# Paddings, earlier fetches, an unprioritised attention and a sum on GpSimd in a two-layer decoder step

## The chip, the cores and the metric

The kernel runs on one NeuronCore of a Trainium2 chip. The metric is the device time of one execution in microseconds; a kernel's number is the median of its runs. A core has five engines with their own instruction queues: TensorE (PE) for matrix products, with weight loads shown apart as PEld; VectorE (DVE); ScalarE (ACT); GpSimd (POOL); and SyncE (SP), which here issues nearly all DMA transfers.

## The reference

One inference step of a trunk with two layers, in fp32, for a prompt of 16 meta tokens and 256 tokens and for a sample group of 8 sequences with one new token each: 280 tokens in all. D is 2048, the branch width 4096, heads have 64 values. Cut to what matters:

```python
# layer A (RWKV-7), xm = token-shifted mixes of rmsnorm(h)
r, k, v, z = rkvz products of 2048 x 4096 each
kk = k * k_k;  kk = kk / max(sqrt(sum(kk * kk, over each head)), 1e-12)
S = S * d - (S kk) b^T + v k^T;  y = S r            # per token and head
y = groupnorm(y) * gn_g + gn_b + sum(r * k * r_k) * v
h = h + (y * silu(z)) @ w_out
# shared K/V, then layer B: window of 128, 64 query heads on 8 K/V heads, one sink per head
k, v = split(rmsnorm(h, kv_norm) @ w_kv);  k = rotary(k)
q, z = split(rmsnorm(h, b_norm) @ b_w_qz);  q = rotary(q)
m = max(max(s), sink);  p = exp(s - m) / (sum(exp(s - m)) + exp(sink - m))
h = h + ((p @ v) * silu(z)) @ b_w_o
y = rmsnorm(h, final_norm)
```

The sample group attends to a cache of 128 keys and values per sequence and K/V head and returns the cache moved on by one.

## The kernel before

**Products.** Every large product is computed to near fp32 from operands split in two: `hi` is the value rounded to the fast format (fp32r), `lo` the rest. `mm3` (lines 199 to 201) issues three TensorE products per block: weight-hi by input-hi, weight-hi by input-lo, weight-lo by input-hi. Tokens are the moving side (280 columns, 264 in layer B, where the meta tokens are dropped), the weights the stationary 128x128 side. `wunits` brings the weights in units of 256 KB: a DMA on SP into a `raw` tile (line 192), a cast on ACT to `whi` (line 177), a subtraction on DVE to `wlo` (line 178). There are 4 `raw` buffers, 4 more (`rawx`) once a wider pool is open, and 5 of `whi` and `wlo`. `gate_tiles` splits the gated branch in the same way, eight tiles `at[g]` of 128x1056 into `ghi` and `glo`, as the input of an output product.

**Order of the work.** TensorE's order is written by hand. `drive` runs a generator of products, six TensorE products to each `yield` (a *position*), and between positions it advances *streams* that emit other work: a stream's `yield n, condition` says how many positions to wait and for what. What a stream emits on TensorE stands in TensorE's queue exactly there. The instructions of the other engines and the DMA issues are put into their queues by a scheduler that simulates the program and has a priority per instruction; `drive` emits the second stream under a priority raised by 2000, the others at the normal one. Once made, each queue runs in order.

**Stages.** In the trace: layer A's products with the chunked recurrence (64 tokens a chunk) in the streams, to about 1345 us; the rest of layer A's output product, to 1460; the shared K/V (`phase_b`), to 1518; layer B's q and z products with the attention of 8 groups in the stream `heads` (`phase_b2`, `products_b`), then z products alone, to 2015; the output product `out_b`, to 2211; final norm and output.

**Names that the change touches.** `ps_kk` (lines 484 and 777): sums of squares of k per head, as two accumulating fp32 products whose stationary side `sel` has 4 columns of a selection matrix; the result stands in 4 rows. An fp32 product shows as two records of the trace. `ps_yt` (line 1210): transpositions of the recurrence's result Y, three blocks of tokens per head pair, 128, 128 and 16 rows. `ps_vt` (lines 488 and 794) transposes v in the other direction, with 128, 128 and 16 columns. `km` (line 843): a factor of k, on ACT. `snk`, `snd` (lines 1490 and 1495): the sinks, spread over partitions, one load and eight small ones. `kc`, `vc` (lines 1706 and 1707): the cached keys and values of one K/V head, and with them the copies that move the output cache on (line 1711), four issues per group, emitted by `attend_cache` at the start of each group. `scores_b`, `softmax` (DVE and ACT, ending in the scaling `P<-P,sm`, line 1667), `turned` (transpositions of P, `ps_pt`, line 1676) and `values` are a half group's attention; `heads` runs 16 of these pairs. `end_z` (line 1545 on) makes the gated branch of one 128-column plane out of a z product. In `out_b`, h is the sum of product and residual (line 1784), `ps_h` its transposition (line 1787), `ht` the scaled result, `junk` and `ss` its squares summed along a row by ACT (line 1792), `rsf` the row's sum and then its root's inverse.

Of the kernel before, what the change touches and what calls it, by code (L numbers as in the profile page):

```python
# [103 lines left out]
class Kernel:  # L104
# [9 lines left out]
    def run(self):  # L114
        nc, tc = self.nc, self.tc
        with contextlib.ExitStack() as st:
# [32 lines left out]
            self.close("gB", "st1", "wx1", "g0", "at", "res")  # L149
# [92 lines left out]
    def params(self):  # L242
# [27 lines left out]
        for off, n in ((C_SEL, 8), (C_BO, 128)):  # L270
            self.cr[off] = self.cp.tile([128, n], F32, name=f"cr{off}")
            dma(self.cr[off], I['consts'][:, off:off + n])
        self.sel = self.cr[C_SEL]
# [194 lines left out]
    def proj(self, m, x, pairs, dst, gemm=None):  # L468

        nc = self.nc  # L470
        for p0 in pairs:
# [5 lines left out]
            for j, ps in enumerate(pss):  # L477
                nc.scalar.copy(t[:, j], ps)
                if m == 1:
                    sq = self.sp.tile([128, N], F32, tag="sqp", bufs=1, name=f"sqp{p0}_{j}")  # L480
                    nc.scalar.activation(sq, ps, AF.Square, scale=self.pcol(P_KK, p0 + j))
                    if j == 0:
                        pk = self.bank(self.py, f"ps_kk{p0}")
                    nc.tensor.matmul(pk[:4, :N], self.sel[:, 4 * j:4 * j + 4], sq, start=j == 0, stop=j == 1)
# [79 lines left out]
    def drive(self, products, streams, begun):  # L564
# [5 lines left out]
        with self.pe_order():  # L570
            while more or self.later or len(live) > 1:
                for s in list(live):
                    if s[1] <= self.pos and (s[2] is None or s[2]()):
# [3 lines left out]
                        try:  # L577
                            with self.tc.high_priority(offset=2000 if s[0] is now[1] else 0), turn:
# [190 lines left out]
    def end_k(self, p0, t):  # L769
# [6 lines left out]
        for j in range(2):  # L776
            nc.tensor.matmul(pk[:4, :N], self.sel[:, 4 * j:4 * j + 4], sq[:, j], start=j == 0, stop=j == 1)
# [22 lines left out]
    def prep(self, u):  # L800
# [41 lines left out]
        for j in range(2):  # L842
            km = rp.tile([128, N], F32, tag="km", name=f"km{j}_{u}")
# [348 lines left out]
    def group_norm(self, o):  # L1192
# [10 lines left out]
        for j in range(4):  # L1203
# [4 lines left out]
            for c in range(3):  # L1208
                r = 128 if c < 2 else 16
                nc.tensor.transpose(ps[:, 128 * c:128 * c + r], Y[:r, c, j].rearrange("p q i -> p (q i)"),  # L1210
                                    self.ident[:r, :r])
# [193 lines left out]
    def phase_b(self):  # L1405
# [11 lines left out]
        self.Vn = t([128, NKV, 2, 64], "Vn")  # L1417
        G.memset(self.Vm, 0.0)
# [60 lines left out]
    def phase_b2(self):  # L1479
# [9 lines left out]
        snk = t([128, 64], "snk")  # L1489
        dma(snk, I['b_sinks'].to_broadcast((128, 64)))  # L1490
        snd = t([128, NKV], "snd")
        G.memset(snd, 0.0)
        with nc.allow_non_contiguous_dma(reason="64 values"):
            for s in range(NS):
                dma(snd[8 * s:8 * s + 8], I['b_sinks'][0].rearrange("(g h) -> h g", h=8))
        self.snk, self.snd = snk, snd
# [8 lines left out]
        self.drive(self.products_b(), [idle(), self.heads()], {})  # L1505
# [42 lines left out]
    def end_z(self, g, pl, ps):  # L1548
# [10 lines left out]
        V.scalar_tensor_tensor(at, zr, 0.5, at, op0=MU, op1=MU)  # L1559

    def heads(self):

        last = None
        for n in range(16):
            g, i = divmod(n, 2)
            if i == 0:
                cache = self.attend_cache(g)
                next(cache)
# [4 lines left out]
            P = [self.softmax(g, 2 * i + a, ps) for a, ps in enumerate(cur)]  # L1573
            yield 4, self.after(3, ('q', g, 3))
            next(cache)
# [3 lines left out]
            next(cache, None)  # L1579
            yield 3  # L1580
# [8 lines left out]
        self.st1 = self.open("st1", side="right", reuse_waits="tile")  # L1589
        self.plan_states(self.st1, 12, [*range(10, 42, 8), *range(64, 176, 7)], 5)  # L1590

# [175 lines left out]
    def out_b(self):  # L1767
        nc, pool, I, O = self.nc, self.gp, self.I, self.O
        V, A = nc.vector, nc.scalar
        gates = [self.gate_tiles(pool if g else self.gp0, NB, g, self.at[g]) for g in range(8)]  # L1770
# [5 lines left out]
        ss = pool.tile([128, 3, KT], F32, name="ss")  # L1776
        V.memset(ss, 0.0)
        for k in range(KT):
# [5 lines left out]
            V.tensor_tensor(h, ps, self.hT[:, k, NM:], op=ALU.add)  # L1784
            pt = self.bank(self.pe, f"ps_h2_{k}")
            for i, r in enumerate(rows):
                nc.tensor.transpose(pt[:r, 128 * i:128 * i + 128], h[:, 128 * i:128 * i + r], self.ident)  # L1787
            for i, r in enumerate(rows):
                s = slice(128 * k, 128 * k + 128)
                V.tensor_tensor(ht[i][:r, s], pt[:r, 128 * i:128 * i + 128], fn[:r, s], op=ALU.mult)  # L1790
                j = pool.tile([128, 128], F32, tag="junk", bufs=2, name=f"junk{k}_{i}")
                A.activation(j[:r], pt[:r, 128 * i:128 * i + 128], AF.Square, accum_out=ss[:r, i, k:k + 1])
        rs = pool.tile([128, 3], F32, name="rsf")
        V.reduce_sum(rs, ss, axis=AX.X)
# [34 lines left out]
```

## Time and profile before

| | |
|---|---|
| median of 3 runs | 2229.13 us (2228.17 to 2234.97) |
| profiled execution, its own time | 2228.68 us |
| its span, first to last instruction | 2226.9 us |
| mean granted TensorE clock | 0.989 |
| busy: PE, PEld, DVE, ACT, POOL | 96%, 90%, 77%, 58%, 3% |
| moved by DMA | 455.40 MB, 205 GB/s mean |

How to read the rows: a timeline row has its start and length in us, the engine, the line of the kernel, the operation, the tile written and the tiles read, the tile's shape (for PE and PEld first rows*columns of the stationary side) and how many such instructions stand in a row; in brackets stands how long the engine was idle before and what ended that. `SPq` is the queue of SP: the length of its rows is the time until the next instruction could be issued. A group's row has its count, busy time and mean in ns, then the idle time before. The granted clock is the share of TensorE's full speed.

### The profile page before, as it was taken

To read this page: it belongs to the slowest core of one execution; us is meant where nothing else is said; L and a number is where in the kernel's file an instruction comes from. 1 tells how busy PE (TensorE), PEld (TensorE's weight loads), DVE (VectorE), ACT (ScalarE), POOL (GpSimd) and SP (SyncE) were. 2 spreads that over 40 slices of the span, in tenths; PEclk is the share of its full clock that TensorE was granted. 3 is DMA by queue.
4 is the path that set the end of the run, shared out by engine and by line. 5 is a ranking of instruction groups with operands and counts; after the bars stand their busy time and mean duration, and the time that the engine had idled before them with its cause. 6 is when DMAs were issued, how large, how long until landed. Compare 5 with 4: busy or idle time off the path is not lost. (4 is left out here: it accounts for less than half of the span.)

```text
span 2226.9 us, 56386 instructions
## 1 busy us (share of the span) xinstructions
PE 2129.4 (96%) x21584; PEld 2000.4 (90%) x21584; DVE 1715.0 (77%) x4136; ACT 1295.2 (58%) x3041; POOL 63.4 (3%) x86
## 2 busy tenths in 40 slices
PE   6999999999999999999999999998999999999997
PEld 4898888899899898989989999998989999999997
DVE  5875757787777777788887787996878888778785
ACT  3546766677666666667666454564556555545443
POOL 0010000000000000000100000100000000000000
PEclk9999999999999999999999999998999999999998
DMA  7978577668666766866656768766544544576773
GB/s 240 339 257 251 179 225 217 201 177 263 211 199 189 225 210 198 262 210 183 194 164 199 242 203 263 242 189 195 153 141 138 169 126 143 165 218 218 229 226 129
DMA packets 424887, 455.40 MB, mean 205 GB/s; under 512 B 64281, under 2 KB 383321, under 8 KB 424225
## 3 DMA queue, kind: packets, MB, share of 16 engines
q1 hardware_dynamic: 423800, 449.51, 65.1%
q8 instruction: 169, 2.77, 0.5%
q10 hardware_dynamic: 816, 2.29, 0.3%
q14 instruction: 102, 0.83, 0.1%
HBM read 385.09 MB, written 70.73 MB: 205 GB/s over the span
## 5 line engine op out<-in xcount | busy, mean ns | idle before, releaser
L199 PE MATMUL ps_q<-bmh,whi_qb 128*128 128x264 f32 x512 | 151.9, 297 | 8.0 <-ACT whi_qb L177 7.9
L199 PE MATMUL ps_z<-mhlm,whi_z 128*128 128x280 f32 x512 | 159.2, 311 | 0.0
L201 PE MATMUL ps_z<-mhlm,wlo_z 128*128 128x280 f32 x512 | 150.2, 293 | 0.5 <-DVE wlo_z L178 0.4
L201 PE MATMUL ps_q<-bmh,wlo_qb 128*128 128x264 f32 x512 | 147.6, 288 | 3.0 <-DVE wlo_qb L178 3.0
L200 PE MATMUL ps_z<-mhlm,whi_z 128*128 128x280 f32 x512 | 150.0, 293 | 0.0
L201 PE MATMUL ps_z<-bmh,wlo_zb 128*128 128x264 f32 x512 | 146.4, 286 | 2.7 <-DVE wlo_zb L178 2.7
L199 PE MATMUL ps_z<-bmh,whi_zb 128*128 128x264 f32 x512 | 148.2, 289 | 0.8 <-ACT whi_zb L177 0.8
L201 PE MATMUL ps_ob<-ghi,wlo_ob 128*128 128x264 f32 x512 | 145.5, 285 | 3.1 <-DVE wlo_ob L178 3.1
L200 PE MATMUL ps_q<-bml,whi_qb 128*128 128x264 f32 x512 | 146.8, 287 | 0.0
L200 PE MATMUL ps_ob<-glo,whi_ob 128*128 128x264 f32 x512 | 144.6, 283 | 1.3 <-DVE glo L178 1.3
L200 PE MATMUL ps_z<-bml,whi_zb 128*128 128x264 f32 x512 | 145.6, 284 | 0.0
L199 PE MATMUL ps_ob<-ghi,whi_ob 128*128 128x264 f32 x512 | 144.9, 284 | 0.0
L178 DVE TENSOR_TENSOR wlo_r<-raw_r,whi_r 128x512 fp32r<-128x512 f32 x128 | 86.9, 686 | 58.3 <-ACT whi_r L177 56.1
L177 ACT CAST whi_oa<-raw_oa 128x512 fp32r<-128x512 f32 x128 | 78.6, 622 | 88.7 <-DMA raw_oa<-a_w_out 29.9
L178 DVE TENSOR_TENSOR wlo_v<-raw_v,whi_v 128x512 fp32r<-128x512 f32 x128 | 87.4, 689 | 51.4 <-ACT whi_v L177 45.6
L177 ACT CAST whi_ob<-raw_ob 128x512 fp32r<-128x512 f32 x128 | 79.1, 621 | 78.1 <-PE ps_ob L200 59.3
L199 PE MATMUL ps_v<-mhlm,whi_v 128*128 128x280 f32 x384 | 121.7, 317 | 0.2 <-ACT st L734 0.2
L199 PE MATMUL ps_k<-mhlm,whi_k 128*128 128x280 f32 x384 | 118.8, 309 | 0.0
L178 DVE TENSOR_TENSOR wlo_k<-raw_k,whi_k 128x512 fp32r<-128x512 f32 x112 | 76.6, 690 | 53.8 <-ACT whi_k L177 49.7
L177 ACT CAST whi_zb<-raw_zb 128x512 fp32r<-128x512 f32 x128 | 78.4, 622 | 65.0 <-PE ps_z L200 45.3
L178 DVE TENSOR_TENSOR wlo_z<-raw_z,whi_z 128x512 fp32r<-128x512 f32 x128 | 87.8, 690 | 36.7 <-ACT whi_z L177 36.3
L200 PE MATMUL ps_v<-mhlm,whi_v 128*128 128x280 f32 x384 | 112.2, 292 | 0.0
(473 smaller groups left out, 7707.1 us busy)
## 6 DMA issues: line engine op xcount, KB each, us to landing
raw_k<-a_w_rkvz SPq DMA_DIRECT2D x128, 256.0 KB
raw_v<-a_w_rkvz SPq DMA_DIRECT2D x128, 256.0 KB
raw_r<-a_w_rkvz SPq DMA_DIRECT2D x128, 256.0 KB
raw_z<-a_w_rkvz SPq DMA_DIRECT2D x128, 256.0 KB
raw_oa<-a_w_out SPq DMA_DIRECT2D x128, 256.0 KB
raw_qb<-b_w_qz SPq DMA_DIRECT2D x128, 256.0 KB
raw_zb<-b_w_qz SPq DMA_DIRECT2D x128, 256.0 KB
raw_ob<-b_w_o SPq DMA_DIRECT2D x128, 256.0 KB
```

The source lines that it names most:

```text
L177: self.nc.scalar.copy(hi, src)
L178: return self.nc.vector.tensor_tensor(lo, src, hi.bitcast(F32), op=ALU.subtract)
L199: mm(ps, wh, xh, start=start, stop=False)
L200: mm(ps, wh, xl, start=False, stop=False)
L201: return mm(ps, wl, xh, start=False, stop=stop)
```

## The change

It has five parts.

1. **Layer A.** `sel` becomes two windows, 128 columns wide, on a 130-column tile that is zero (memset on GpSimd) but for two columns; the `ps_kk` products now write 128 rows, of which 4 are read as before. The third transposition of `ps_yt` takes all 128 rows of Y and writes 128 columns, of which 16 are read. `km` uses the buffers of tag `sq`.
2. **Sinks and caches.** The nine loads of the sinks and a memset move from `phase_b2` to the start of `phase_b`. The first cache set is requested 12 positions into layer B's products; each later one at the end of the group before.
3. **Attention.** `drive` has a parameter `ahead`, 0 for layer B, so that `heads` has no priority. The second softmax of a pair is emitted four positions later, behind the `yield 4`.
4. **Gates.** A third stream, `gates_b`, splits the tiles `at[0]` to `at[4]` while the last z products run, each four positions behind its z planes; 5 to 7 stay in `out_b`.
5. **Final squares.** In `out_b` one Square of h on ACT per 128 columns of D replaces three reads of `ps_h` with a sum each; GpSimd adds the squares up in `sqacc`, and six small products with a column of ones (`ps_stb`) sum over the partitions at the end. Three instructions on DVE take the place of a reduction and one instruction.

```diff
+        selt = self.cp.tile([128, 130], F32, name="selt")
+        nc.gpsimd.memset(selt, 0.0)
+        dma(selt[:, 2:4], I['consts'][:, C_SEL:C_SEL + 2])
+        self.sel = [selt[:, 2:130], selt[:, 0:128]]
...
-            nc.tensor.matmul(pk[:4, :N], self.sel[:, 4 * j:4 * j + 4], sq[:, j], start=j == 0, stop=j == 1)
+            nc.tensor.matmul(pk[:, :N], self.sel[j], sq[:, j], start=j == 0, stop=j == 1)
...
-            km = rp.tile([128, N], F32, tag="km", name=f"km{j}_{u}")
+            km = rp.tile([128, N], F32, tag="sq", bufs=2, name=f"km{j}_{u}")
...
-                r = 128 if c < 2 else 16
-                nc.tensor.transpose(ps[:, 128 * c:128 * c + r], Y[:r, c, j].rearrange("p q i -> p (q i)"),
-                                    self.ident[:r, :r])
+                nc.tensor.transpose(ps[:, 128 * c:128 * c + 128], Y[:, c, j].rearrange("p q i -> p (q i)"), self.ident)
...
+        self.snk, self.snd = t([128, 64], "snk"), t([128, NKV], "snd")
+        dma(self.snk, I['b_sinks'].to_broadcast((128, 64)))
+        G.memset(self.snd, 0.0)
+        with nc.allow_non_contiguous_dma(reason="64 values"):
+            for s in range(NS):
+                dma(self.snd[8 * s:8 * s + 8], I['b_sinks'][0].rearrange("(g h) -> h g", h=8))
...
-        self.drive(self.products_b(), [idle(), self.heads()], {})
+        self.drive(self.products_b(), [idle(), self.heads(), self.gates_b()], {}, 0)
...
     def heads(self):
-        last = None
+        last, cache = None, self.attend_cache(0)
+        yield 12
+        next(cache)
         for n in range(16):
             g, i = divmod(n, 2)
-            if i == 0:
-                cache = self.attend_cache(g)
-                next(cache)
             yield (5 if n else 0), self.after(3, ('q', g, 2 * i + 1))
             cur = [self.scores_b(g, 2 * i + a) for a in range(2)]
             if last:
                 self.values(*last)
-            P = [self.softmax(g, 2 * i + a, ps) for a, ps in enumerate(cur)]
+            P = [self.softmax(g, 2 * i, cur[0])]
             yield 4, self.after(3, ('q', g, 3))
+            P.append(self.softmax(g, 2 * i + 1, cur[1]))
             next(cache)
             yield 8
             T = [self.turned(g, 2 * i, P[0])]
             yield 2
             next(cache, None)
+            if i and g < 7:
+                cache = self.attend_cache(g + 1)
+                next(cache)
...
+    def gates_b(self):
+        self.gates = []
+        for g in range(5):
+            yield 3, self.after(4, ('h', 7), ('z', g))
+            self.gates.append(self.gate_tiles(self.g1 if g else self.gp0, NB, g, self.at[g]))
...
-        gates = [self.gate_tiles(pool if g else self.gp0, NB, g, self.at[g]) for g in range(8)]
+        gates = self.gates + [self.gate_tiles(pool, NB, g, self.at[g]) for g in range(5, 8)]
...
+            sq = pool.tile([128, NB], F32, tag="sqb", bufs=2, name=f"sqb{k}")
+            A.activation(sq, h, AF.Square)
+            if k == 0:
+                acc = pool.tile([128, NB], F32, name="sqacc")
+                nc.gpsimd.tensor_copy(acc, sq)
+            elif k < KT - 1:
+                nc.gpsimd.tensor_tensor(acc, acc, sq, op=ALU.add)
...
-                A.activation(j[:r], pt[:r, 128 * i:128 * i + 128], AF.Square, accum_out=ss[:r, i, k:k + 1])
+            if k >= KT - 2:
+                for i, r in enumerate(rows):
+                    nc.tensor.matmul(pst[i][:r, 0:2], (acc if k == KT - 2 else sq)[:, 128 * i:128 * i + r], one,
+                                     start=k == KT - 2, stop=k == KT - 1)
...
-        V.reduce_sum(rs, ss, axis=AX.X)
-        V.tensor_scalar(rs, rs, 1.0 / D, EPS, op0=ALU.mult, op1=ALU.add)
+        for i, r in enumerate(rows):
+            V.tensor_scalar(rs[:r, i:i + 1], pst[i][:r, 0:1], 1.0 / D, EPS, op0=ALU.mult, op1=ALU.add)
```

How the queues change is seen in three places. The first is SP's queue at the start of layer B's products, between two loads of q weights (`raw_qb`). Before:

```order
L192 DMA raw_qb_2_23367<-b_w_qz 128x2x256
L1706 DMA kc_23233<-cache_k 128x8x64
L1707 DMA vc_23234<-cache_v 128x8x64
L1711 DMA s_cache_k<-cache_k 16x4064
L1711 DMA s_cache_v<-cache_v 16x4064
...
L1468 DMA s_cache_v<-Vn 8x8x64
L1490 DMA snk<-b_sinks 128x64
L1495 DMA snd<-b_sinks 8x8x1 x8
L192 DMA raw_qb_4_23379<-b_w_qz 128x2x256
```

Left out are the second cache set, four issues as in the first, and two of three transfers of K/V results: 20 issues in all stand between the two weights. After the change:

```order
L192 DMA raw_qb_2_23368<-b_w_qz 128x2x256
L1470 DMA Vm<-Vm 16x8x64
L1473 DMA p_cache_v<-Vd 128x512
L1475 DMA s_cache_v<-Vn 8x8x64
L1719 DMA kc_23362<-cache_k 128x8x64
L1720 DMA vc_23363<-cache_v 128x8x64
L1724 DMA s_cache_k<-cache_k 16x4064
L1724 DMA s_cache_v<-cache_v 16x4064
L192 DMA raw_qb_4_23380<-b_w_qz 128x2x256
```

Seven issues are left there; three more weights (`raw_qb_6`, `raw_qb_8`, `raw_qb_10`) follow, and only then the second cache set. The sinks' nine issues now stand in the K/V stage, behind `constb` and ahead of the next loads of K/V weights.

The second is ACT's queue at the turn from the z products (`thb` is `end_z`'s Tanh) to the output product (`whi_ob`). Before:

```order
L1556 ACTIVATE thb_2_30294<-zr_2_30292 128x264
L177 CAST whi_ob_6_30411<-raw_ob_6_30409 128x512
L177 CAST whi_ob_8_30441<-raw_ob_8_30439 128x512
L177 CAST ghi_30330<-at_23195 128x1056
L177 CAST ghi_30334<-at_23196 128x1056
L177 CAST ghi_30338<-at_23197 128x1056
L177 CAST ghi_30342<-at_23198 128x1056
L177 CAST ghi_30346<-at_23199 128x1056
L177 CAST ghi_30350<-at_23200 128x1056
L1556 ACTIVATE thb_3_30312<-zr_3_30310 128x264
```

After:

```order
L1555 ACTIVATE thb_2_30318<-zr_2_30316 128x264
L177 CAST whi_ob_6_30418<-raw_ob_6_30416 128x512
L177 CAST whi_ob_8_30448<-raw_ob_8_30446 128x512
L177 CAST ghi_30350<-at_23212 128x1056
L177 CAST ghi_30354<-at_23213 128x1056
L1555 ACTIVATE thb_3_30336<-zr_3_30334 128x264
```

Six gate casts in a row have become two; gates 1 to 4 stand earlier, among the casts of the z weights, and the last comes eight casts later.

The third is TensorE's queue at the end, after the change (`h_14` and `h_15` are the last two blocks of h):

```order
L1808 MATMUL ps_h_14_33011<-consts,h_14_33006 128x128 x2
L1808 MATMUL ps_h_14_33011<-consts,h_14_33006 8x128
L1814 MATMUL ps_stb_30367<-one,sqacc 128x2
L1814 MATMUL ps_stb_30368<-one,sqacc 128x2
L1814 MATMUL ps_stb_30369<-one,sqacc 8x2
L1808 MATMUL ps_h_15_33025<-consts,h_15_33021 128x128 x2
```

The small products that read GpSimd's sum stand between the two groups of transpositions; three that read the last square follow behind them. In layer B's q and z products TensorE's order is the same before and after; on DVE and ACT one to three casts of weights now stand ahead of a softmax's last scalings and exponentials.

More of the change, by code (lines that the diff above doesn't have):

```diff
@@ L148, in run @@
             self.wx = None
-            self.close("gB", "st1", "wx1", "g0", "at", "res")
+            self.close("gB", "g1", "st1", "wx1", "g0", "at", "res")
     def open(self, name, bufs=1, **k):
@@ L269, in params @@
         self.cr = {}
[L270 to L273, printed above, removed]
+        self.cr[C_BO] = self.cp.tile([128, 128], F32, name="crbo")
+        dma(self.cr[C_BO], I['consts'][:, C_BO:C_BO + 128])
+        selt = self.cp.tile([128, 130], F32, name="selt")
+        nc.gpsimd.memset(selt, 0.0)
+        dma(selt[:, 2:4], I['consts'][:, C_SEL:C_SEL + 2])
+        self.sel = [selt[:, 2:130], selt[:, 0:128]]
         self.half = self.cp.tile([128, 2], F32, name="half")
@@ L483, in proj @@
                         pk = self.bank(self.py, f"ps_kk{p0}")
-                    nc.tensor.matmul(pk[:4, :N], self.sel[:, 4 * j:4 * j + 4], sq, start=j == 0, stop=j == 1)
+                    nc.tensor.matmul(pk[:, :N], self.sel[j], sq, start=j == 0, stop=j == 1)
                 if m == 2:
@@ L559, in phase_a, with drive @@
                    {preps: [wait, need]})
-    def drive(self, products, streams, begun):
+    def drive(self, products, streams, begun, ahead=2000):
         self.samples = False
@@ L577, in drive @@
                         try:
-                            with self.tc.high_priority(offset=2000 if s[0] is now[1] else 0), turn:
+                            with self.tc.high_priority(offset=ahead if s[0] is now[1] else 0), turn:
                                 w = next(s[0])
@@ L1488, in phase_b2 @@
         V.tensor_scalar(self.sinr, self.sinr, HD ** -0.5, None, op0=MU)
[L1489 to L1496, printed above, removed]
         self.Pm, self.qz = t([128, 4, 128], "Pm"), [t([128, 576], f"qz{i}") for i in range(2)]
@@ L1588, in heads @@
         self.close("B2")
-        self.st1 = self.open("st1", side="right", reuse_waits="tile")
+        right = dict(side="right", reuse_waits="tile")
+        self.st1 = self.open("st1", **right)
         self.plan_states(self.st1, 12, [*range(10, 42, 8), *range(64, 176, 7)], 5)
+        self.g1 = self.open("g1", **right)
+    def gates_b(self):
[3 more added lines that the diff above has]
+            self.gates.append(self.gate_tiles(self.g1 if g else self.gp0, NB, g, self.at[g]))
     def bx(self, k):
@@ L1775, in out_b @@
         ht = [pool.tile([128, D], F32, name=f"ht{i}") for i in range(3)]
-        ss = pool.tile([128, 3, KT], F32, name="ss")
-        V.memset(ss, 0.0)
+        pst = [self.bank(p, f"ps_stb{i}") for i, p in enumerate((self.pc, self.pp, self.py))]
+        one = pool.tile([128, 2], F32, name="one")
+        V.memset(one, 1.0)
         for k in range(KT):
```

4 lines of the change are left out of this document (3 added, 1 removed).

## The prediction

> **What bounds the kernel now.** I read the page's busy shares first, then a table by stage, then what TensorE (PE) waits for, then the places themselves.
>
> ```profile
> PE 2129.4 (96%) x21584; PEld 2000.4 (90%) x21584; DVE 1715.0 (77%) x4136; ACT 1295.2 (58%) x3041; POOL 63.4 (3%) x86
> 1600.00:1700.00 100.00, 97.30 (x813) 92.94 (x811) 81.31 (x303) 57.09 (x154) 0.00 (x0) 0.98 0.47 143
> 1900.00:2000.00 100.00, 100.00 (x832) 99.40 (x831) 77.89 (x157) 50.92 (x102) 0.00 (x0) 1.00 0.64 191
> ```
>
> In the table a row has the stretch, its length, then busy time of PE, weight loads (PEld), DVE, ACT and GpSimd (POOL), the granted clock, the DMA share and GB/s. TensorE bounds the whole: 96% of the span, 97% in a stretch of the attention, 100% in the gate products. Two things alone can shorten it: less time per PE instruction, or fewer of the short stretches in which PE waits. The change goes after both. Where PE waits, in layer B:
>
> ```profile
> PE ps_z L201 <- DVE wlo_zb L178: 2.7, 4, 1.3
> PE ps_q L201 <- DVE wlo_qb L178: 3.0, 4, 1.3
> PE ps_q L199 <- ACT whi_qb L177: 7.9, 2, 7.5
> PE ps_ob L201 <- DVE wlo_ob L178: 3.1, 1, 3.1
> PE ps_ob L200 <- DVE glo L178: 1.3, 1, 1.3
> ```
>
> (microseconds in all, times, longest). Each names the split of a weight or a gate: ACT rounds it (whi, ghi), DVE subtracts (wlo, glo), and what PE multiplies next is not ready.
>
> **Layer A paddings.** What these cost is read from how long a foreign instruction interrupts the regular products, 0.12 to 0.13 us apart.
>
> ```profile
> 403.91 0.29 PE L201 MATMUL ps_v<-mhlm,wlo_v 128*128 128x280 f32 x1
> 404.50 0.29 PE L200 MATMUL ps_v<-mhlm,whi_v 128*128 128x280 f32 x1
> 408.42 0.29 PE L201 MATMUL ps_v<-mhlm,wlo_v 128*128 128x280 f32 x1
> 408.86 0.13 PEld L1210 LDWEIGHTS ps_yt<-consts,Y 16*128 16x128 f32 x1 [0.17 <-issue]
> 409.26 0.29 PE L200 MATMUL ps_v<-mhlm,whi_v 128*128 128x280 f32 x1
> 329.96 0.29 PE L201 MATMUL ps_k<-mhlm,wlo_k 128*128 128x280 f32 x1
> 331.22 0.19 PEld L199 LDWEIGHTS ps_k<-mhlm,whi_k 128*128 128x128 f32 x1 [0.47 <-issue]
> 331.45 0.29 PE L200 MATMUL ps_k<-mhlm,whi_k 128*128 128x280 f32 x1
> 99.40 0.29 PE L201 MATMUL ps_v<-mv,wlo_v 128*128 128x280 f32 x1
> 99.53 1.10 PE L402 MATMUL ps_a_w<-mst,lw 128*96 128x280 f32 x4
> 100.60 0.29 PE L200 MATMUL ps_v<-mv,whi_v 128*128 128x280 f32 x1
> L794 PEld LDWEIGHTS ps_vt<-consts,st x72: 88/138/143, 403.9 to 928.4; 128*128 128x128 f32 x48, 128*16 128x16 f32 x24
> L1210 PEld LDWEIGHTS ps_yt<-consts,Y x96: 132/138/143, 408.4 to 1350.2; 128*128 128x128 f32 x64, 16*128 16x128 f32 x32
> L777 PEld LDWEIGHTS ps_kk<-sqk,cr x48: 82/86/87, 330.2 to 843.8; 128*4 128x4 f32 x48
> L484 PEld LDWEIGHTS ps_kk<-sqp,cr x16: 82/84/86, 55.3 to 105.7; 128*4 128x4 f32 x16
> ```
>
> The last four rows count loads by shape, rows * columns (nanoseconds least/median/most). From the product before to the second product behind, the three transpositions of a vt group, 128 rows in each load, take 404.50 - 403.91 = 0.59 us; those of a yt group, 16 rows in the third, 409.26 - 408.42 = 0.84 us, and its load stands 0.17 us waiting for nothing shown. I put the 0.25 us on the 16 rows: 32 groups, 8.0 us. The pair of fp32 products with 4 columns takes 331.45 - 329.96 = 1.49 us, the pair with 96 columns 100.60 - 99.40 = 1.20; the load behind the first waits 0.47 us. So 0.29 a pair: 48 loads are 12 pairs (four a pair, as fp32 shows two records each), 3.5 us, and the 16 of phase 0 are 8 single products at, say, the same (each is followed by its own change back), 2.3 us. In all 13.8 us. I take 80%, **-11**: some of these breaks lie shortly ahead of a chain for which PE then waits, and the saving ends there. Against it: the vt group's own third load has only 16 columns and shows no pause, so narrow columns might not be what the pair pays for; that leaves the yt part alone, and two thirds of it are 5. Ends: -14 and -5.
>
> [...]
>
> [...] The memset of the wider matrix (GpSimd, ahead of all) and `km` taking the place of `sq` cost nothing: POOL is 3% busy, and ACT, which does both, 58%.
>
> **Sinks moved into the K/V stage.**
>
> ```profile
> 1463.05 8.43 SPq L192 DMA_DIRECT2D raw_kv<-w_kv  x2
> 1528.95 3.18 SPq L1495 DMA_DIRECT2D snd<-b_sinks  x8
> ```
>
> Nine issues at 3.18 / 8 = 0.40 us are 3.6 us on SP, put in ahead of 1463.05. There two weight loads take 8.43 us to issue, where eight issues took 3.18: they wait for a buffer that an earlier product must free, and that wait covers the nine. **+0.5** for loads a little late; all 3.6 if that cover is gone.
>
> **Start of layer B's products.**
>
> ```profile
> 1518.47 1.73 SPq L1706 DMA_DIRECT2D kc<-cache_k  x1
> 1530.77 0.28 PE L201 MATMUL ps_q<-bmh,wlo_qb 128*128 128x264 f32 x1
> 1532.23 16.04 SPq L192 DMA_DIRECT2D raw_qb<-b_w_qz  x11
> 1537.85 0.62 ACT L177 CAST whi_qb<-raw_qb 128x512 fp32r<-128x512 f32 x1 [4.63 <-DMA raw_qb<-b_w_qz]
> 1538.52 0.59 PE L199 MATMUL ps_q<-bmh,whi_qb 128*128 128x264 f32 x1 [7.48 <-ACT whi_qb L177]
> 1538.00:1548.00 10.00, 8.06 (x32) 7.22 (x33) 7.76 (x24) 7.46 (x24) 0.00 (x0) 0.50 0.43 133
> 1548.00:1558.00 10.00, 10.00 (x84) 10.00 (x84) 7.21 (x20) 4.33 (x7) 0.00 (x0) 1.00 0.65 197
> ```
>
> Twenty issues stand in SP's queue from 1518.47 to 1532.23, 13.76 us or 0.69 each, between two weight loads. The next weight is issued at 1532.23 and lands at 1537.85, 5.6 us later; PE has run dry at 1531.05 and stands 7.48 us, and once more 0.4 (7.9 in two waits, above). Then the clock: 0.50 from 1538 to 1548, 32 products instead of 84. Beside idle time it costs (84 x 0.806 - 32) x 0.12 = 4.3 us, 0.806 being the busy share of that stretch; I take 3.4, as part of that stretch has no product ready anyway. Together 7.9 + 3.4 = 11.3 us. After the change 7 issues stand there, by 0.69 each 4.8 us: the weight is issued at 1523.3 and lands at 1528.9, ahead of 1531.05, so neither the wait nor the lower clock should come. I leave 1.5 us, since the second cache set (4 issues, 2.8 us by 0.69) follows four weights later: **-9.8**, ends -11.3 (all gone) and -4 (the wait cut to half, but the clock still falls).
>
> **The rest of the attention.** The second softmax goes behind four positions, and no instruction is lifted ahead of the casts.
>
> ```profile
> 1863.11 0.55 DVE L1667 TENSOR_SCALAR P<-P,sm 128x128 f32<-128x128 f32 x2
> 1867.60 0.60 PE L1676 MATMUL ps_pt<-consts,P 128*128 128x128 f32 x4
> ```
>
> Beside the start PE waits for DVE's splits 2.7 + 3.0 = 5.7 us in eight places, one of them right behind the start. I read them so: a softmax's instructions, lifted by the priority, overtake the split that PE wants next, and DVE, 81% busy from 1600 to 1700, doesn't catch up in time. Of the 5.7 us I take **-4.5**, ends -6 (a little of the clock with it) and 0: without the lift a burst on DVE remains. What hides the later softmax is its slack: P is ready at 1863.66 and its transposition starts at 1867.60, 3.9 us later, the tightest of those I read. On DVE one to three splits go ahead of it, 0.7 us each, so 2 us of that is used.
>
> **Gates split early.**
>
> ```profile
> 2015.42 5.95 ACT L177 CAST ghi<-at 128x1056 fp32r<-128x1056 f32 x6
> 2021.01 3.59 DVE L178 TENSOR_TENSOR glo<-at,ghi 128x1056 fp32r<-128x1056 f32 x3
> ```
>
> Six casts stand in a row on ACT for 5.95 us, and the weights' splits behind them: PE waits 1.3 + 3.1 = 4.4 us. Four of these move into the gate products, where each is 0.99 us on ACT (50.92 of 100 busy) and 1.2 us on DVE (77.89): the idle 22% covers 4.8 us spread over some 100. Two casts are left at the turn. **-3.5**, ends -4.4 and -1.
>
> **Squares summed on GpSimd.**
>
> ```profile
> 2210.85 0.43 DVE L1784 TENSOR_TENSOR h<-ps_ob,hT 128x264 f32<-128x264 f32 x1 [1.01 <-PE ps_ob L201]
> 2215.04 0.20 DVE L1794 TENSOR_REDUCE rsf<-ss 128x3 f32<-128x48 f32 x1 [0.43 <-ACT junk L1792]
> L1388 POOL TENSOR_TENSOR sqacc<-sqacc,sqa 128x280 f32<-128x280 f32 x14 | 14.4, 1032 | 73.6 <-ACT sqa L1383 73.4
> ```
>
> Only the end counts: in the output products PE waits nowhere but in the two places at the turn, so the work that changes there runs beside PE. If DVE stood through all 14 sums on POOL, some 14.4 us, it would still have time: the idle 22% of the gate products' row, over 196 us, is 43. Before, ACT and DVE take turns on the same banks, the last wait of 0.43 us among them, and the reduction starts 2215.04 - 2211.28 = 3.8 us behind the last h. After, the path is a square (of the size of h, 0.43), three transpositions (as in layer A, 0.59 less the 0.12 of a product), three scalings of half that size, at most 0.3, and three short instructions of 0.2: 2.4 us if none overlaps. The new matmuls for the sum wait for GpSimd's last addition, about 1.03 us, in front of the last transpositions, which gives some back. 3.8 - 2.4 = 1.4, one short instruction less, and a little given back: **-1.5**, ends -2.2 and 0 (an addition of 1.7 us or more).
>
> **Sum.** -11 + 0.5 - 9.8 - 4.5 - 3.5 - 1.5 = -29.8 on the profiled execution's 2228.68: 2198.9, so **2199 us**; the three timed runs have their median 0.45 us higher, which is nothing here.
>
> **Rivals.** (1) The paddings bring nothing:
>
> ```profile
> L893 PEld LDWEIGHTS ps_bo<-rk,cr 128*128 128x128 f32 x64 | 10.0, 188 | 3.6 <-DVE vT L894 1.9 <-DVE ks L779 1.3
> ```
>
> A wide fp32 load in 128 columns is 188 ns in this group, a narrow one 85; if loads stood bare, 64 x 0.10 = +6.6 us, and with the pause kept the paddings end between 0 and +6.6 instead of -11: 2210 to 2217. For it: the 16-column load without a pause; against: the two breaks. (2) The start of B only shifts its stall to the second cache set, or the clock still falls: 4 to 8 us of the 9.8 stay, 2203 to 2207. For it: SP still has 11 issues there that are no weights; against it: four weights now go between them. (3) Both: 2214 to 2225. (4) Slower: without priority the softmax falls behind the splits; PE, in order, stands at `turned`. It decides from a slip over 3.9 us on; with ten splits of 0.69 ahead it is 6.9, a wait of 3 us on each of 15 pairs, +45 against the other terms' -29.8 + 4.5: 2248. Against it stand the one to three splits that moved. (5) The priority was not what made the waits, and gates and tail bring half: 2228.68 - 29.8 + 4.5 + 2.5 = 2206.
>
> **Chances.** The forecast 0.60, (1) 0.11, (2) 0.14, (3) 0.05, (4) 0.04, (5) 0.06. All lower ends together are -37.9, 2191; of the upper ones I let the two largest fall together, -5 and -4 in place of -11 and -9.8, 2211: its own range. Rivals 2 and 5 lie in it and 1 just above, so 2188 to 2216 holds 8 in 10, with the misses of my sizes. A measurement here tells no change apart to about 0.3%, 6.7 us: faster means under 2222.4. All but (4) and about half of (3) fall there: faster 0.92, same 0.04, slower 0.04.
>
> **What would show it.** Paddings: breaks of the yt group near 0.59 us, of the kk pair near 1.2, layer A's end some 11 us earlier. Start: no PE wait over 2 us from 1500 to 1560 (less the shift), granted clock 1.0 there. Attention: PE's waits on `wlo_qb` and `wlo_zb` under 2 us together, none of a transposition of P on DVE. Gates: no wait on `wlo_ob` at the turn. End: the first rsf step at most 2.5 us behind the last h. It would be wrong if breaks stay as they are, or if a softmax row appears as PE's releaser.

## The result, and the profile after

The changed kernel takes 2209.15 us (median of 4 runs, 2203.19 to 2211.88), the kernel before 2232.05 us beside it (4 runs, 2228.17 to 2240.49): the ratio is 0.9885, with a 95% interval of 0.9864 to 0.9907, about 26 us less. Later comparisons, with more runs of the kernel before, put that one at 2234 to 2235 us. The profiled execution of the changed kernel took 2211.88 us, the one of before 2228.68.

The first products of the shared K/V, of q and of the output product mark the stages. In both traces (a tile's instructions: count, least/median/most ns, first and last start), before:

```profile
L199 PE MATMUL ps_kv<-kvh,whi_kv x128: 287/292/399, 1456.8 to 1513.3; 128*128 128x280 f32 x128
L199 PE MATMUL ps_q<-bmh,whi_qb x512: 279/285/586, 1513.7 to 1855.7; 128*128 128x264 f32 x171
L199 PE MATMUL ps_ob<-ghi,whi_ob x512: 278/283/373, 2014.8 to 2210.3; 128*128 128x264 f32 x171
```

and after:

```profile
span 2209.9 us, 56367 instructions
PE 2122.6 (96%) x21596; PEld 2013.0 (91%) x21596; DVE 1711.5 (77%) x4138; ACT 1283.1 (58%) x2961; POOL 76.1 (3%) x102
L199 PE MATMUL ps_kv<-kvh,whi_kv x128: 287/291/399, 1462.6 to 1520.5; 128*128 128x280 f32 x128
L199 PE MATMUL ps_q<-bmh,whi_qb x512: 279/284/422, 1520.9 to 1846.5; 128*128 128x264 f32 x171
L199 PE MATMUL ps_ob<-ghi,whi_ob x512: 278/283/378, 2004.8 to 2195.3; 128*128 128x264 f32 x171
```

From the first K/V product to the end it is 2226.9 - 1456.8 = 770.1 us before and 2209.9 - 1462.6 = 747.3 after: 22.8 us less behind layer A. Layer A itself ended 5.8 us *later* in this execution, though it was to end 11 us earlier. Both halves need an answer. Matching every product of one trace with the same product of the other gives the shift along the way:

```
at (trace of before)     shift of the same product in the changed kernel
 393 us  layer A          +0.8
 444     layer A          +5.6
1457     shared K/V       +5.8
1519     first q products +7.2     K/V stage  +1.4
1596     q, attention     -1.2     start      -8.4
1920     z alone          -10.0    attention  -8.9
2044     output product   -14.9    gates      -4.9
2227     end              -17.0    tail       -2.1
```

**Layer A's breaks** are as short as forecast (timeline; a product, the foreign instruction, the second product behind):

```profile
409.23 0.29 PE L201 MATMUL ps_v<-mhlm,wlo_v 128*128 128x280 f32 x1
409.36 0.49 PE L1212 MATMUL ps_yt<-consts,Y 128*128 128x128 f32 x3
409.82 0.29 PE L200 MATMUL ps_v<-mhlm,whi_v 128*128 128x280 f32 x1
330.79 0.29 PE L201 MATMUL ps_k<-mhlm,wlo_k 128*128 128x280 f32 x1
330.92 1.11 PE L780 MATMUL ps_kk<-sqk,selt 128*128 128x280 f32 x4
332.00 0.29 PE L200 MATMUL ps_k<-mhlm,whi_k 128*128 128x280 f32 x1
L780 PEld LDWEIGHTS ps_kk<-sqk,selt x48: 188/189/190, 330.8 to 849.3; 128*128 128x128 f32 x48
```

A yt group takes 0.59 us (0.84 before), a kk pair 1.21 (1.49), and over all such breaks the median is 0.59, 1.20 and, for the single kk products of phase 0, 0.73 (1.02). The kk loads did become longer, 189 ns for 86, and the break shorter all the same.

**Layer B's waits** are nearly gone. PE's list of waits between 1500 us and the end of the z products, after, and the granted clock in the stretches that answer to those before:

```profile
PE ps_q L199 <- ACT whi_qb L177: 1.8, 1, 1.8
PE ps_q L201 <- DVE wlo_qb L178: 1.1, 3, 0.5
...
1540.00:1560.00 20.00, 17.30 (x127) 16.66 (x126) 15.35 (x52) 10.90 (x31) 0.00 (x0) 0.91 0.62 187
1600.00:1700.00 100.00, 99.77 (x853) 96.04 (x852) 84.40 (x311) 58.84 (x155) 0.00 (x0) 1.00 0.51 156
2000.00:2030.00 30.00, 30.00 (x249) 30.00 (x249) 26.85 (x47) 16.30 (x27) 0.73 (x2) 1.00 0.81 258
```

The waits on `wlo_zb`, `whi_zb`, `glo` and `wlo_ob` (2.7, 0.8, 1.3, 3.1 us) no longer appear. What is left stands at the start. SP's queue there, and ACT where PE waits:

```profile
1526.10 0.92 SPq L1470 DMA_DIRECT2D Vm<-Vm  x1
1531.11 2.38 SPq L192 DMA_DIRECT2D raw_qb<-b_w_qz  x4
1535.54 2.13 ACT L177 CAST whi_qb<-raw_qb 128x512 fp32r<-128x512 f32 x3 [5.08 <-DMA raw_qb<-b_w_qz]
1541.62 0.40 ACT L1671 ACTIVATE P<-P,mx 128x144 f32<-128x144 f32 x1
1545.19 2.16 ACT L177 CAST whi_qb<-raw_qb 128x512 fp32r<-128x512 f32 x4
1545.84 0.39 PE L199 MATMUL ps_q<-bmh,whi_qb 128*128 128x264 f32 x1 [1.78 <-ACT whi_qb L177]
```

Seven issues take 5.0 us, the weight behind them is cast at 1535.54, and PE doesn't miss it. It misses the weights after those: eight exponentials of the first softmax pair stand on ACT from 1541.62 to 1545.19 ahead of four casts.

At the end, the step that begins the inverse root (`rsy`, behind `rsf`) comes 2.2 us behind the last h, where it came 2215.48 - 2211.28 = 4.2 us behind it. Before:

```profile
2215.48 0.17 DVE L290 TENSOR_SCALAR rsy<-rsf 128x3 int32<-128x3 int32 x1
```

After:

```profile
2195.54 0.74 POOL L1805 TENSOR_TENSOR sqacc<-sqacc,sqb 128x264 f32<-128x264 f32 x1 [21.32 <-ACT sqb L1800]
2195.90 0.43 DVE L1798 TENSOR_TENSOR h<-ps_ob,hT 128x264 f32<-128x264 f32 x1 [1.01 <-PE ps_ob L201]
2196.34 0.73 PE L1814 MATMUL ps_stb<-one,sqacc 128*128 128x2 f32 x6 [0.15 <-POOL sqacc L1805]
2197.00 0.55 PE L1808 MATMUL ps_h<-consts,h 128*128 128x128 f32 x3
2198.49 0.17 DVE L293 TENSOR_SCALAR rsy<-rsf 128x3 int32<-128x3 int32 x1
```

### The profile page after: what moved, and what is told of

It reads as the page before. It is cut to its first block, busy times and chain, and to the rows that moved or that the text cites. A ratio compares the mean times of both kernels' runs of the same rounds, so it can differ in the third digit from the quotient of the medians.

```text
span 2209.9 us, 56367 instructions
## 1 busy us (share of the span) xinstructions
PE 2122.6 (96%) x21596; PEld 2013.0 (91%) x21596; DVE 1711.5 (77%) x4138; ACT 1283.1 (58%) x2961; POOL 76.1 (3%) x102
## 5 line engine op out<-in xcount | busy, mean ns | idle before, releaser
L199 PE MATMUL ps_v<-mhlm,whi_v 128*128 128x280 f32 x384 | 122.5, 319 | 0.7 <-ACT whi_v L177 0.7
L201 PE MATMUL ps_v<-mhlm,wlo_v 128*128 128x280 f32 x384 | 113.2, 295 | 0.2 <-DVE wlo_v L178 0.2
```

Source lines behind the costliest of these rows:

```text
L199: mm(ps, wh, xh, start=start, stop=False)
L201: return mm(ps, wl, xh, start=False, stop=stop)
```

## Experiments on layer A: where 13 us of shorter breaks went

The theories: the paddings pay what their breaks show and one execution hid it (P, with C for the chance); moving `km` on DVE and ACT costs it (O); most of it comes back in layer A as waits and half clock (S). The runs from here on stand on four chips. The kernel before, timed beside them, has medians of 2234.0 (twice), 2234.6 and 2235.3 us there, so differences of 1 to 2 us between runs are not read.

**The changed kernel again**, no edit.

> The changed kernel, unaltered, as the yardstick for the others of this job and to see how much of layer A's loss repeats. In its first profile the widened loads shorten every break as forecast (0.59 for 0.84 us, 1.20 for 1.49, 0.73 for 1.02: 13 us in all), and yet the shared K/V begins 5.8 us later than before: PE waits 7 us more in layer A and stands at half clock in six windows more of 3.4 us, of which the stretch from 390 to 435 us alone costs 5. Theory C (chance: a late transfer in the chain of k's norms delayed SP's queue in that one execution): the shift at the shared K/V differs by more than 4 us between the two profiles, and here it is -5 to -11. Theory O (order: the instructions with km, moved ahead on DVE and ACT, hold up the splits): the shift is again +4 to +8. Time of both: 2203 to 2212.

Measured: 2206.53 us (5 runs, 2205.45 to 2208.89), ratio to before 0.9886 (0.9867 to 0.9906). In this trace the shared K/V begins at 1458.8, 2 us later than in the trace of before. So the shift differed by 3.8 us between two executions of one program, but it is neither the -5 to -11 of theory C nor the +4 to +8 of theory O. In six executions with the same layer A that stage ended between 1453.1 and 1462.6; in four without the paddings between 1456.8 and 1471.1. One cause of the spread is seen at 393 to 435 us: the transfer `kx<-kr` in the chain of k's norms reaches DVE at 397.8 in the trace of before, at 399.6 in the first of the changed kernel, and between 395.4 and 400.5 in the others. The issues behind it in SP's queue, weights among them, move with it.

**Without the paddings.** The whole first part is undone, the selection matrix with its memset, both uses of it, the transposition and km's tag:

```diff
-        self.sel = [selt[:, 2:130], selt[:, 0:128]]
+        self.sel = self.cr[C_SEL]
...
-            nc.tensor.matmul(pk[:, :N], self.sel[j], sq[:, j], start=j == 0, stop=j == 1)
+            nc.tensor.matmul(pk[:4, :N], self.sel[:, 4 * j:4 * j + 4], sq[:, j], start=j == 0, stop=j == 1)
...
-                nc.tensor.transpose(ps[:, 128 * c:128 * c + 128], Y[:, c, j].rearrange("p q i -> p (q i)"), self.ident)
+                r = 128 if c < 2 else 16
+                nc.tensor.transpose(ps[:, 128 * c:128 * c + r], Y[:r, c, j].rearrange("p q i -> p (q i)"),
+                                    self.ident[:r, :r])
```

> The changed kernel without its first part: the selection matrix has 4 columns again, the third transposition 16 rows, km its own buffers; parts 2 to 5 stay. Theory P (the paddings pay as forecast, and only chance hid it): slower than the changed kernel by 8 to 13 us, 2217 to 2222. Theory O (they pay 13 us in breaks, but moving km costs 15 to 19): faster than the changed kernel by 3 to 6 us, 2203 to 2206. Theory S (layer A is bound by chains and by the delivery of weights, so that shorter breaks come back as waits): the same as the changed kernel within 3 us.

Measured: 2209.35 us (5 runs, 2205.58 to 2212.44), ratio 0.9896 (0.9876 to 0.9915): 2.8 us slower than the changed kernel on the same chip. That is theory S's answer; P's 8 to 13 and O's gain are outside it.

**The yt part alone** (the last change of that diff is left as it is in the changed kernel, the others undone), and **km alone** on the kernel before:

```diff
-            km = rp.tile([128, N], F32, tag="km", name=f"km{j}_{u}")
+            km = rp.tile([128, N], F32, tag="sq", bufs=2, name=f"km{j}_{u}")
```

> The changed kernel with only the third transposition of its first part (16 rows made 128); selection matrix and km as before. Theory P: 5 to 8 us faster than without any padding. Theory O: the same 5 to 8 us, and so 8 to 14 us faster than the changed kernel, 2195 to 2201. Theory S: within 3 us of both.

> The kernel before with one edit: km uses the buffers of tag sq. TensorE's queue is the same row by row; on DVE and ACT the products with km move ahead of one to three splits. Theory O: 10 to 19 us slower than before (2242 to 2251), with new waits and half-clock windows between 390 and 435 us. Theories P, C and S: the same as before within 3 us.

Measured: yt alone 2205.84 us (4 runs, 2203.48 to 2210.47), 0.7 us under the version with the rest of the paddings and 3.5 under the one without, near theory S's 3 and not theory P's 5 to 8. km alone 2233.51 us (12 runs), ratio to before 1.0007 (0.9993 to 1.0020): theory O has fallen. Its one profiled execution happened to be its slowest, 2243.37 us, and shows the same new waits and half-clock windows at 417 and 431 us as the first trace of the changed kernel, where they last 3.4 us each. Without the timed runs that trace would have proved the wrong theory.

**The paddings on the kernel before**, the first part of the change as its diff shows it, and nothing else.

> The kernel before with the whole first part of the change (selection matrix of 128 columns, third transposition of 128 rows, km in the buffers of sq) and nothing else. So far the changed kernel with and without this part differs by 3 us where its breaks are 13 us shorter. Theory S (most of a shorter break comes back as a wait or as half clock in layer A): 1 to 5 us faster than before. Theory P (the paddings pay 8 to 13 us, and the earlier pair of runs was spread): 2221 to 2226. In the profile the time of layer A's products less PE's waits and half-clock loss is 12 us shorter than before in either case.

Measured: 2229.89 us (12 runs) against 2234.6 (17 runs), ratio 0.9981 (0.9967 to 0.9994): by the ratio 4.2 us faster, 1.3 to 7.4. Theory S's size. Layer A from 190 us to its end, in windows (length, then PE, PEld, DVE, ACT, POOL; clock; DMA), in three traces: the kernel before, the changed kernel without the paddings, and the kernel before with the paddings:

```profile
190.00:1456.80 1266.80, 1228.15 (x14509) 1144.69 (x14508) 980.76 (x2149) 802.41 (x1871) 51.86 (x61) 0.99 0.69 213
```

```profile
190.00:1462.80 1272.80, 1230.73 (x14504) 1146.95 (x14504) 979.21 (x2149) 799.02 (x1868) 51.53 (x61) 0.99 0.69 212
```

```profile
190.00:1455.50 1265.50, 1222.23 (x14503) 1151.54 (x14503) 977.98 (x2148) 797.29 (x1864) 51.38 (x61) 0.99 0.69 212
```

The shorter breaks do stand in the trace. PE's busy time there, less half of the time at half clock (20.5, 23.9 and 31 us; before's q products stand 0.22 us apart at 0.50, at 1546 us, and 0.12 at 1.00, at 1549), is 1218, 1219 and 1207 us: 11 to 12 us less with the paddings, as expected. PE's idle time is 38.7 and 42.1 us without, 43.3 us with them. It is 41.2 on average in four traces without the first part (38.7 to 44.1) and 44.1 in seven with all of it (41.2 to 45.5): some 3 us came back as waits, read from ranges that overlap. The clock can be read from every timed run: 0.9847 on average in the 12 runs with the paddings, 0.9867 in the 17 runs of before. As time at half clock that is 2 x (1 - clock) x 2225, 68 against 59 us, with a standard error of some 2.3 us in the difference, and about half of the 9 is lost: 4.4 us. By the medians above the breaks are shorter by 32 x 0.246 + 12 x 0.286 + 8 x 0.289 = 13.6 us, and 13.6 - 3 - 4.4 = 6 us should be left of them; 4.2 were measured, with an interval that holds both.

**More work instead of less.** If layer A simply had slack that any saving falls into, added work should fall into it too.

```diff
-        for j in range(2):
+        for j in (0, 1, 0, 1):
             nc.tensor.matmul(pk[:, :N], self.sel[j], sq[:, j], start=j == 0, stop=j == 1)
```

> The changed kernel with each pair of kk products in layer A's stream issued twice into the same bank (the second pair starts the sum anew, so the result is the same): 12 times two more fp32 products, by the pair's 1.20 us less one product of 0.13 and a half about 0.95 us each, 11 us more work on TensorE, all of it in layer A between 330 and 850 us. Theory S: 2 to 6 us slower than the changed kernel, as the waits of chains shrink in return. Theory P: 10 to 12 us slower.

Measured: 2217.92 us (6 runs, 2217.06 to 2222.51), 11.4 us over the changed kernel: theory P's answer, and theory S's 2 to 6 missed. Added work counts in full. So theory S holds for the size of the loss but not in that simple form: the added time shortened no wait (PE's idle time in layer A is 45 us there too). Why shorter breaks draw waits and half-clock windows after them, and longer ones don't take them away, no run here tells; a chain that ends at a fixed number of products after its start, and so has less time when those are faster, would fit the first half, but this was not tried.

## Experiments on layer B: which edit made the gain

Theory Q says that the priority made the waits, theory F that the earlier requests and the later second softmax took them away.

**The priority put back.**

```diff
-        self.drive(self.products_b(), [idle(), self.heads(), self.gates_b()], {}, 0)
+        self.drive(self.products_b(), [idle(), self.heads(), self.gates_b()], {}, 2000)
```

> The changed kernel with the raised priority of the attention put back (ahead 2000), all else as changed. TensorE's queue stays the same row by row; in SP's queue both cache sets stand again ahead of the fourth q weight, 11 issues and no weight between them. Theory Q (the priority is what made the waits in layer B): the start loses 3 to 6 us and the attention the 5 to 9 us that it gained, 2215 to 2221, with PE waiting for wlo_qb and wlo_zb 4 us or more. Theory F (the earlier requests and the later second softmax made the gain): within 2 us of the changed kernel.

Measured: 2212.41 us (6 runs, 2207.90 to 2215.87), 5.9 us slower than the changed kernel, between the times of the two theories. The old waits are back, nearly word for word:

```profile
PE ps_q L201 <- DVE wlo_qb L178: 3.1, 5, 1.3
PE ps_z L201 <- DVE wlo_zb L178: 2.7, 4, 1.3
PE ps_q L199 <- ACT whi_qb L177: 0.7, 1, 0.7
PE ps_z L199 <- ACT whi_zb L177: 0.7, 1, 0.7
```

Behind the start, the same products lose 7.4 us against the changed kernel. The start itself lost nothing; it was 1.7 us shorter, although 11 issues stand there and not 7: PE waited 0.7 us for the weight behind them and 1.0 for a later split, and no window at half clock came (no q product takes over 392 ns). So half of theory Q's expectation, the start, missed.

**The softmaxes together, the caches late.**

```diff
-            P = [self.softmax(g, 2 * i, cur[0])]
+            P = [self.softmax(g, 2 * i + a, ps) for a, ps in enumerate(cur)]
             yield 4, self.after(3, ('q', g, 3))
-            P.append(self.softmax(g, 2 * i + 1, cur[1]))
```

```diff
-        last, cache = None, self.attend_cache(0)
-        yield 12
-        next(cache)
+        last = None
...
             g, i = divmod(n, 2)
+            if i == 0:
+                cache = self.attend_cache(g)
+                next(cache)
...
-            if i and g < 7:
-                cache = self.attend_cache(g + 1)
-                next(cache)
```

> The changed kernel with the second softmax of a pair emitted right behind the first again, ahead of the yield of 4. Theory Q: within 2 us of the changed kernel. Theory F: 4 to 9 us slower, with the waits on wlo_qb and wlo_zb back.

> The changed kernel with each cache set requested at the start of its group, as before. SP's queue at the start of layer B comes out the same as in the changed kernel: the requests are placed by priority, not by where they are emitted. Theory Q: within 2 us of the changed kernel. Theory F: the start's 8 us come back in part, 3 us slower or more.

Measured: 2205.34 us (4 runs) and 2207.21 us (5 runs), 1.2 less and 0.7 more than the changed kernel. Neither edit makes the gain. SP's queue is the same with the requests late, since priority and due time place them there and not the line that emits them. So that run tests the line of the request, not a later place in the queue.

**The sinks late.** The six lines that load them go from `phase_b` back to `phase_b2`:

```diff
         self.Vn = t([128, NKV, 2, 64], "Vn")
-        self.snk, self.snd = t([128, 64], "snk"), t([128, NKV], "snd")
-        dma(self.snk, I['b_sinks'].to_broadcast((128, 64)))
...
         V.tensor_scalar(self.sinr, self.sinr, HD ** -0.5, None, op0=MU)
+        self.snk, self.snd = t([128, 64], "snk"), t([128, NKV], "snd")
+        dma(self.snk, I['b_sinks'].to_broadcast((128, 64)))
```

> The changed kernel with the sinks' nine loads back at the start of layer B's products. In SP's queue 16 issues instead of 7 then stand ahead of the fourth q weight, some 3.6 us more by 0.40 each. Theory D (the weight behind them sets when PE may start): the wait at the start grows by 2 to 4 us and a second half-clock window comes (1.5 us), while the shared K/V loses 1 to 1.5 us less: 1 to 4 us slower. Theory N (the weights at the start are early enough either way): 1 to 1.5 us faster than the changed kernel.

Measured: 2206.28 us (5 runs, 2203.47 to 2211.69), no difference in the timed runs. The trace shows both halves of the exchange. The K/V stage is 56.9 us long again, 1.4 less, and at the start one long wait returns (beside two of 0.2 us), behind 16 issues of 11.6 us:

```profile
1514.77 0.76 SPq L1464 DMA_DIRECT2D Vm<-Vm  x1
1518.06 3.00 SPq L1495 DMA_DIRECT2D snd<-b_sinks  x8
1526.38 2.06 SPq L192 DMA_DIRECT2D raw_qb<-b_w_qz  x4
```

```profile
PE ps_q L199 <- ACT whi_qb L177: 3.9, 1, 3.9
```

From the first K/V product to the end that execution took 748.4 us, 1.0 more than the changed kernel's 747.4. Theory D has the mechanism, its size is too small for the timed runs.

**The priority alone taken from the kernel before.**

> The kernel before with one edit: the attention of layer B is emitted without its priority. In SP's queue 16 issues, not 20, then stand ahead of the fourth q weight, as with the sinks late in the changed kernel. Theory Q, sized by the runs so far: the rest of the attention gains 5 to 9 us; the start, 16 issues long, goes from some 13 us of waits and half clock to the 7 of the run with the sinks late, 4 to 6 us; together 9 to 15 us faster than before, 2219 to 2225, and q and z products (first of them to the first output product) 486 to 491 us instead of 501. Theory F (the gain needs the earlier requests of caches and sinks): less than 5 us.

```diff
-    def drive(self, products, streams, begun):
+    def drive(self, products, streams, begun, ahead=2000):
...
-                            with self.tc.high_priority(offset=2000 if s[0] is now[1] else 0), turn:
+                            with self.tc.high_priority(offset=ahead if s[0] is now[1] else 0), turn:
...
-        self.drive(self.products_b(), [idle(), self.heads()], {})
+        self.drive(self.products_b(), [idle(), self.heads()], {}, 0)
```

Measured: 2221.72 us (6 runs, 2217.61 to 2222.81), ratio 0.9938 (0.9920 to 0.9956), 13.6 us less than before: theory Q's answer, and half of the whole change from one number. Its waits from 1500 to 2100 us:

```profile
PE ps_q L199 <- ACT whi_qb L177: 4.2, 1, 4.2
PE ps_ob L201 <- DVE wlo_ob L178: 3.1, 1, 3.1
PE ps_ob L200 <- DVE glo L178: 1.3, 1, 1.3
PE ps_q L201 <- DVE wlo_qb L178: 0.2, 1, 0.2
```

The start is shorter by 5.7 us (one wait of 4.2 for 7.5 and two small ones, and 6.8 us at half clock for 13.7), the attention by 9.3, and the gates' two waits stand as before. For the weight behind the issues PE waited 7.5 us with 20 of them ahead of it, 3.9 and 4.2 with 16, 0.7 with 11, and not at all with 7. Once it comes in time, fewer issues gain nothing.

**A version from these findings**: the softmaxes together, and the sinks loaded while the rest of layer A's output product runs.

```diff
         for k in range(KT):
+            if k == 4:
+                self.tc.keep_in_program_order(self.nc.sync.dma_start(self.snk, self.I['b_sinks'].to_broadcast((128, 64))))
...
```

> The changed kernel with the second softmax of a pair again right behind the first, and with the sinks' nine loads issued in the rest of layer A's output product, where SP waits for buffers, into tiles of the constants' pool. From the lengths of the stages after layer A: 2 us by the softmax (745.3 for 747.3 us from the shared K/V to the end) and 1.4 us by the shared K/V (58.3 back to 56.9): 3 us faster than the changed kernel, 2202 to 2205. If the nine issues only move their lateness into the output product, it is 0 to 2 us.

Measured: 2205.88 us (4 runs, 2203.14 to 2208.38), ratio 0.9870 (0.9850 to 0.9891). The K/V stage came back to 56.7 us as expected, but from the first K/V product to the end it is 746.2 us, 1.1 less than the changed kernel and not 3: a half-clock window stood in the K/V stage (products of up to 436 ns by `whi_kv`, 399 in the changed kernel), beside the one at the start that the changed kernel has too. Three versions, this one, the yt part alone and the softmaxes together, have medians 0.7, 0.7 and 1.2 us under the changed kernel's 2206.53, which their spread of 2 to 7 us does not tell apart. No faster kernel than the changed one is shown.

## Why the prediction was right, and where it was not

The forecast was 2199 us (2188 to 2216) and faster; measured are 2209 and, again, 2207. The gain of 29.8 us was 25.7, 21 to 30 by the interval. That the sum came near is in part luck. Its largest term fell some 7 us short and the base was 5 us low, while attention, gates and tail gave 6.4 us more than forecast.

- **Paddings, -11: measured -3 to -4.** The step that failed is "I take 80%". The reading of the breaks was right to 0.01 us, and a fifth for breaks ahead of a waiting chain was far too little: two thirds of 13.6 us came back (6 to 12 us by the interval), some 3 as waits and some 4 through the granted clock, which the sum did not consider for layer A at all. Why a shorter break draws them stays open. The rival "the paddings bring nothing" was near by its time, and wrong by its mechanism. It had loads standing bare: they did go from 86 to 189 ns, and the breaks became shorter (1.49 to 1.20 us a pair). So the longer load was covered here, while the pause behind the narrow one (0.47 us for the kk pair) was not. What makes the pause is not settled: the 16-column load of the vt group has none.
- **The profiled execution as base.** "0.45 us higher, which is nothing here" was wrong. Over 17 runs before has its median at 2234, 5 us over the profiled execution, and layer A alone moves by 5 us or more from one execution to the next. With 2234 as the base the same sum gives 2204.
- **Sinks, +0.5: +1.4.** The nine issues take 4.0 us there, and the cover that was named holds the larger part:

```profile
1468.30 0.42 SPq L1420 DMA_DIRECT2D snk<-b_sinks  x1
1468.82 3.57 SPq L1424 DMA_DIRECT2D snd<-b_sinks  x8
1473.21 3.82 SPq L192 DMA_DIRECT2D raw_kv<-w_kv  x2
```

- **Start, -9.8: -8.4.** The issue, landing and PE's need came as worked out (5.0 us for the seven issues, 4.8 forecast). What remained, 1.8 us of wait and a window of 3.4 us at half clock, was put on the second cache set; the rows show eight exponentials on ACT. And the credit went to the wrong edit in part: not the place of the requests but the priority kept two cache sets ahead of the weight.
- **Attention, -4.5: -8.9.** The cause was right, and the run with the priority back shows it. The caution was not: all waits behind the start went, and with them a half-clock window (3.4 us from 1629.9 before) and smaller stalls that the list of waits doesn't hold. The slack of the later softmax was sized wrongly as well. The tightest after the change is 1.3 us, not the 1.9 that 3.9 less 2 gives, and it lies at another pair, which had 5.5 us before:

```profile
1625.62 0.54 DVE L1680 TENSOR_SCALAR P<-P,sm 128x128 f32<-128x128 f32 x2
1627.48 0.82 PE L1689 MATMUL ps_pt<-consts,P 128*128 128x128 f32 x6
```

  It is 1.3 there too with the softmaxes together and in the kernel before without the priority, so the missing priority takes that slack and not the later softmax.

  The rival that is slower, a softmax too late for PE, had its condition nearer than the 0.04 sounded, and it did not come.
- **Gates, -3.5: -4.9.** Both waits are gone, and the two casts left at the turn cost nothing. In the kernel before without the priority these waits drew a window of 3.4 us at half clock (at 2018.8 us); in the trace of before they drew none. No run takes the gates or the tail alone. From the first output product to the end it is 205.1 to 206.2 us in all ten traces that have both and 212.1 to 213.6 in the four that have neither, so the 7 us of the two together are shown.
- **Tail, -1.5: -2.1.** GpSimd's last addition took 0.74 us where 1.03 was assumed, which fits, but no run tests it alone.

## What to carry to other kernels

A priority that lifts a side stream over the split of the next operand can cost the bounding engine a small wait again and again, eight here; where the side stream has microseconds of slack, emitting it at the normal priority was worth 14 us in the kernel before, more than any other edit that was tried alone (6 in the changed one, where the sinks were out of the way). Shorter breaks between products are not yet a shorter stage: in a stage held by chains, as layer A, with 20.5 us at a granted clock of 0.50 in the trace of before and 41.0 in that of after, measure what one such edit brings before the rest is added up. And one profiled execution is a sample: give its distance to the median of many runs, and check a difference in one trace against the timed runs before it gets a cause.

## What the hardware showed that was not expected

In the traces of the kernel before and of the changed one, up to the end of the output products, the granted clock stands at 0.50 for 3.4, 6.8 or 13.7 us at a time. From 190 us on each of these stretches begins within 4.4 us of the start of an idle time of TensorE of 0.9 us or more, but the length of one wait does not tell whether one comes. At the start of layer B's products a wait of 1.2 us drew none (the softmaxes together: no q product takes over 391 ns, where at half clock they take 420), one of 1.8 us drew 3.4 us (the changed kernel), waits of 3.9 and 4.2 us drew 6.8 (the sinks late; the kernel before without the priority), and 7.5 us with 1.0 behind drew 13.7 (the kernel before). Elsewhere in the kernel before, idle times of 1.7 us at 272 us and 2.2 at 424 drew none, while 1.8 us at 835 and 1.3 at 1628 had 3.4 us each behind them, from 838.0 and 1629.9. The gates' two waits, 1.3 and 3.1 us, drew none there, and a window in the kernel before without the priority. What decides it, no run here shows.

A stationary operand of 4 columns, or of 16 rows, cost TensorE 0.29 us more per pair of products and 0.25 us more per group of transpositions here than one of 128 by 128 (1.49 for 1.20, 0.84 for 0.59), though its own load took no longer (86 ns for 189, and 132 to 143 ns for both). One with 16 columns in the vt group's transpositions cost nothing extra (0.59).
